# Other read orders behind four groups of head matmuls, and a later second use of x's first block

## The chip, the cores and the metric

The kernel runs on one core of one Trainium2 chip. The metric is the time of one execution in device microseconds (us); the time given for a kernel is the median of its runs. A profile is one execution, recorded by the hardware profiler; its span goes from the first to the last instruction.

## The reference

A trunk of one attention layer with a residual and two RMS norms, in float32, for x of 256 rows and 4096 columns, 32 heads of 128. (The second, convolutional layer of the file is not reached: DEPTH is 1.)

```python
h = x
xn = rms_norm(h, norm_attn)
q, k, v, g = split(xn @ w_in_attn, 4)          # 4096 x 16384
# per head, strictly causal, scale = 1/sqrt(128):
z = q @ k.T * scale
log_fail = where(causal, log_sigmoid(-z), 0)
suffix = reverse_cumsum(log_fail) - log_fail
a = where(causal, exp(log_sigmoid(z) + suffix), 0)
o = a @ v
h = h + (o * silu(g)) @ w_out_attn              # 4096 x 4096
out = rms_norm(h, final_norm)
```

## The kernel before, in words

The two large products are cut into units. The 16 units of the first (u = 0 to 15) each hold 256 columns of q, k, v and gate, so two heads; the units behind them hold the columns of the output product. A unit goes through 16 steps of 256 rows of the weights. In a step a scheme of Strassen's kind, with seven block products in place of eight in some steps, is applied; unit 0 and the first output unit use plain blocks (eight). Each block product is three matmuls of 512 columns in a rounded float32 (`mm3`): the operands are split into a high and a low part, and high x high, high x low and low x high are added up in one PSUM bank. The weights' parts are made per step, the high by a cast on ScalarE (`wh`), the low by a subtraction on VectorE (`wl`, line of `piece`). The parts of x (`forms`, `sh` and `sl`) are made once in unit 0 for that unit's plain blocks (`blocks_of`) and extended there by sums of blocks for the mixed units (`sums_of`).

`mm3` takes for each of the three matmuls a letter. The letter says in which order the 512 columns of the moving operand are read and those of the bank written: "e" reads runs of eight columns, 32 columns apart, in four passes; "c" reads runs of four, 16 apart, in four passes; three letters are a word, the word of one product. All orders give the same sum for each column. Which word a product gets is decided in `product`: the first products behind a group of other matmuls take the words of a list, one after the other; apart from that the first product of a step takes "ecc", and every other "eee".

The groups of other matmuls are those of the heads. A head has four: turn (transposes of q and k), scores, scan (the running sums) and values, two heads to a unit, in the order turn, scores, scan, values of head 0, then of head 1. They are put between the products of the next unit as soon as their inputs are there. In the middle of the run the products that follow them up to the next group are 3 (turn 0), 9 (scores 0), 9 (scan 0), 4 (values 0), 4 (turn 1), 8 (scores 1), 8 (scan 1) and 72 (values 1).

The order of instructions on each engine is written out when the kernel is built, by a planner (`Plan`) that simulates the engines: work asks for an engine with a cost and a key (its due time), the engine takes the waiting work with the lowest key when it is free, and what it takes is emitted in that order. So the order within an engine is fixed and a late instruction holds up those behind it. All instructions therefore show one line in the profile, L135; they are told apart by the names of their tiles. `yield nc.until(name)` lets a piece of planned work sleep until another has told that name: it changes the order, and adds no semaphore by itself.

For x's first block (i = 0) `blocks_of` makes the high and low forms in two cuts, since the first products wait for them. Then it scales the block by the gain (2 ScalarE instructions of 256 columns), subtracts its halves (256 columns on VectorE) and splits the differences into two parts (`differences`, `both_parts`), for use from unit 1 on; with that the block's buffer ("one") is given back, and the load of block 4 can take it. The name ("low", 2, 0) is told when the low of part 2, the first part of step 1 of unit 0, is planned to be done.

Of the kernel before, what the change touches and what calls it, by code (L numbers as in the profile page):

```python
# [19 lines left out]
P = 128  # L20
# [7 lines left out]
NB = D // CW  # L28
# [6 lines left out]
RUNS = {"e": (4, 8), "c": (4, 4), "g": (2, 8)}  # L35
BEHIND_OTHERS = ("ccc", "ecc", "eee", "eee", "eee", "eee", "ecc")
IN_STEP = ("ecc", "ecc")
BEHIND = {}
WARM, WARM_SHORT, IDLE = 10, 5, 640


# [70 lines left out]
def tensor_ns(n):  # L112
    return 0.4167 * n + 8.5 if n > 128 else 109.0
# [138 lines left out]
def kernel(  # L252
# [10 lines left out]
    nc = Plan(tc)  # L263
# [14 lines left out]
    def minus(out_, full, part):  # L278
        nc.vector.tensor_tensor(out=out_, in0=full, in1=part.bitcast(F32), op=ALU.subtract)
# [49 lines left out]
    def soon(c=4.0):  # L329
        return nc.here + 1e3 * c  # L330
# [13 lines left out]
    FULL_P, FULL_S = (P,) * 2, (W,) * 2  # L344

    since_others, words = 0, BEHIND_OTHERS

    def ten(emit, *n, what):
        def others():
            nonlocal since_others, words  # L350
            first_ = BEHIND.get(what, ())
            since_others, words = 0, first_ + BEHIND_OTHERS[len(first_) :]
            emit()

        return nc.work("tensor", 40 + sum(tensor_ns(m) for m in n), others, nc.here - 1e4, wait=400)
# [209 lines left out]
    def blocks_of(i):  # L565

        key = place_of[0, i]
        tag = ("one", "two", "s", "s")[i % 4]
        yield nc.take(tag)
        pool, inside, bufs = (wp, "s", SINGLES) if tag == "s" else (ap, tag, 1)  # L570
        y = pool.tile([P, KT, S], F32, tag=inside, name=f"xs{i}", bufs=bufs)
        y4 = y.rearrange("p k (a b) -> p (k a) b", a=NT)
        h, l = new_forms(i, "s")
        gain = lambda c: gcol[:, i * KT + c : i * KT + c + 1]
        if i:
            yield moved(
                "sync", lambda: nc.sync.dma_start(y, xT[i]), [KT * S], key - 1, hold=True, wait=1300 * i - 600 if i < 4 else 0
            )

            def scaled():  # L580
                for c in range(KT):
                    nc.scalar.activation(y[:, c, :], y[:, c, :], AF.Copy, scale=gain(c))
                nc.scalar.copy(h[:, 0:4, :], y4)

            yield act(scaled, (S, S, 2 * S), key - 2e3)
            yield dve(lambda: minus(l[:, 0:4, :], y4, h[:, 0:4, :]), 2 * S, key)
        else:
            yield moved("scalar", lambda: nc.scalar.dma_start(gcol, gain_in), [KC], key - 1)
            yield moved("scalar", lambda: nc.scalar.dma_start(y, xT[i]), [KT * S], key - 1, hold=True)
            for c in range(KT):  # L590
                hc, lc = (t[:, 2 * c : 2 * c + 2, :].rearrange("p a b -> p (a b)") for t in (h, l))

                yield dve(
                    lambda: nc.vector.tensor_scalar(out=hc, in0=y[:, c, :], scalar1=gain(c), scalar2=None, op0=ALU.mult),
                    S, key - 1,
                )
                nc.tell(("sh", c))
                yield nc.until(("low", 0, c))
                yield dve(
                    lambda: nc.vector.scalar_tensor_tensor(  # L600
                        out=lc, in0=y[:, c, :], scalar=gain(c), in1=hc.bitcast(F32), op0=ALU.mult, op1=ALU.subtract
                    ),
                    S, key - 1,
                )
        nc.tell(("form", "s", i))
        later = place_at(0, i + BLOCKS_LATER)
        if not i:

            def scaled():
                for c in range(KT):  # L610
                    nc.scalar.activation(y[:, c, :], y[:, c, :], AF.Copy, scale=gain(c))

            yield act(scaled, (S, S), later)
        yield from sums_of(i, y4, "n", later)
        nc.give(tag)
# [214 lines left out]
    BW = 3 * P  # L830
    not_before = off.broadcast_to([P, 2, P])

    def head(u, i):
        act_ = lambda *w: act(*w, soon(4.0 if u else HEADS_FIRST))
        yield nc.take("att", "gh", sooner=True)
        tr = att.tile([P, 2, S], F32, tag="att", name=f"tr{u}_{i}")

        def turn():
            for k in range(2):
                for t in range(NT):  # L840
                    c = k * CW + i * P
                    nc.tensor.transpose(tr[:, k, t * P : (t + 1) * P], st["qk", u][:, t, c : c + P], ident)

        yield ten(turn, P, P, P, P, what=("turn", i))
        if i == HG - 1:
            nc.give("one")
        qk = wp.tile([P, 2, S], F32, tag="gh", name=f"qkT{u}_{i}", bufs=ROWS)
        yield act_(lambda: nc.scalar.copy(qk, tr), 2 * S)
        nc.give("att")
        yield nc.take("att", sooner=True)  # L850
        bank = att.tile([P, W], F32, tag="att", name=f"z{u}_{i}")
        z, gT = bank[:, 0:BW], bank[:, BW:W]

        def turned(to, t):
            nc.tensor.transpose(to, st["gv", u][:, t, i * P : (i + 1) * P], ident)

        def scores():
            kw = dict(stop=False, skip_group_check=True)
            nc.tensor.matmul(z[:, 0:P], qk[:, 1, P:S], qk[:, 0, P:S], start=True, **kw)
            nc.tensor.matmul(z[:, P:BW], qk[:, 1, 0:P], qk[:, 0, :], start=False, **kw)  # L860
            diagonal = z[:, 0 : 2 * P].rearrange("p (a b) -> p a b", a=2)
            nc.tensor.matmul(diagonal, ident_b, not_before, start=False, **kw)

        yield ten(scores, *FULL_P, *FULL_S, 2 * P, what=("scores", i))
        nc.give("gh")
        yield nc.take("gh", sooner=True)

        f = wp.tile([P, BW], F32, tag="gh", name=f"f{u}_{i}", bufs=ROWS)

        def soft():  # L870
            nc.scalar.activation(f, z, AF.Softplus, scale=scale)
            nc.scalar.activation(f, f, AF.Copy, scale=1.0 / scale)

        yield act_(soft, (BW + TABLE, BW))
        yield nc.take("gh", "gh", sooner=True)
        fh, fl = (wp.tile([P, BW], F32R, tag="gh", name=f"f{k}{u}_{i}", bufs=ROWS) for k in "hl")
        yield act_(lambda: nc.scalar.copy(fh, f), BW)
        yield dve(lambda: minus(fl, f, fh), BW)
        nc.give("gh")

        if i == 0:
            yield nc.until(("gate", u))

        def scan():
            kw = dict(start=False, skip_group_check=True)
            nc.tensor.matmul(z, neg_tri, fh, stop=False, **kw)
            nc.tensor.matmul(z, neg_tri, fl, stop=False, **kw)
            nc.tensor.matmul(z[:, 2 * P : BW], neg_one, fh[:, 0:P], stop=False, **kw)
            nc.tensor.matmul(z[:, 2 * P : BW], neg_one, fl[:, 0:P], stop=True, **kw)
            turned(gT, 0)  # L890

        yield ten(scan, BW, BW, P, P, P, what=("scan", i))
        nc.give("gh", "gh")
        gated = st["gv", u][:, :, i * P : (i + 1) * P]
        yield nc.take("gh", sooner=True)
        a = wp.tile([P, BW], F32, tag="gh", name=f"a{u}_{i}", bufs=ROWS)


        def weights_of():
            nc.scalar.activation(a, z, AF.Relu, scale=-scale)  # L900
            nc.scalar.activation(a, a, AF.Exp, scale=-1.0)

        yield act_(weights_of, (BW, BW + TABLE))
        yield act_(lambda: nc.scalar.copy(gated[:, 0, :], gT), P)
        nc.give("att")
        yield nc.take("att", sooner=True)
        bank2 = att.tile([P, BW], F32, tag="att", name=f"o{u}_{i}")
        o, gT2 = bank2[:, 0:S], bank2[:, S:BW]
        v = lambda t: st["gv", u][:, t, CW + i * P : CW + (i + 1) * P]

        def out_of_head():
            kw = dict(skip_group_check=True)
            nc.tensor.matmul(o, v(0), a[:, P:BW], start=True, stop=False, **kw)
            nc.tensor.matmul(o[:, P:S], v(1), a[:, 0:P], start=False, stop=True, **kw)
            turned(gT2, 1)

        yield ten(out_of_head, *FULL_P, *FULL_S, P, what=("values", i))
        nc.give("gh")
        yield act_(lambda: nc.scalar.copy(gated[:, 1, :], gT2), P)
        o2 = o.rearrange("p (t b) -> p t b", t=NT)  # L920
        yield dve(lambda: nc.vector.tensor_tensor(out=gated, in0=o2, in1=gated, op=ALU.mult), S)
        nc.give("att")
# [444 lines left out]
```

## Time and profile before

| what | value |
|---|---|
| median of 3 runs | 1682.7 us (1682.67 to 1683.74) |
| the profiled execution's own time | 1683.75 us |
| its span | 1681.7 us |
| TensorE (PE) busy | 1666.9 us, 99% |
| VectorE (DVE) busy | 1611.1 us, 96% |
| ScalarE (ACT) busy | 1265.1 us, 75% |
| mean DMA rate | 249 GB/s |
| mean granted TensorE clock | 0.997 |

Matmuls are pipelined: the time from one's start to the next's is shorter than the duration of one in its row, so the pace is read from the starts. Rows name the tiles: `acc` are the products, `tr`, `z` and `o` the heads' matmuls, `xs` x's blocks, `sh` and `sl` their forms, `raw`, `wh` and `wl` the weights and their parts. A bracket behind a row says how long the engine stood idle before it and what released it. The letters of the words are not in the rows; they follow from the code.

### The profile page before, as it was taken

To read this page: it belongs to the slowest core of one execution; us is meant where nothing else is said; L and a number is where in the kernel's file an instruction comes from. 1 tells how busy PE (TensorE), PEld (TensorE's weight loads), DVE (VectorE), ACT (ScalarE), POOL (GpSimd) and SP (SyncE) were. 2 spreads that over 40 slices of the span, in tenths; PEclk is the share of its full clock that TensorE was granted. 3 is DMA by queue.
4 is the path that set the end of the run, shared out by engine and by line. 5 is a ranking of instruction groups with operands and counts; after the bars stand their busy time and mean duration, and the time that the engine had idled before them with its cause. 6 is when DMAs were issued, how large, how long until landed. Compare 5 with 4: busy or idle time off the path is not lost.

```text
span 1681.7 us, 25051 instructions
## 1 busy us (share of the span) xinstructions
PE 1666.9 (99%) x7736; PEld 1410.1 (84%) x7736; DVE 1611.1 (96%) x1851; ACT 1265.1 (75%) x1665; POOL 366.0 (22%) x448
## 2 busy tenths in 40 slices
PE   9999999999999999999999999999999999999997
PEld 7888888888888888888888888888888888888885
DVE  9899999999999999999999999999999978999997
ACT  8896868686868696968686868686878766665664
POOL 0022222222222222222222221222222112212110
PEclk9999999999999999999999999999999999999998
DMA  9978898989897989797989897979898978888895
GB/s 340 350 187 255 228 253 226 263 221 261 225 265 212 271 209 279 199 282 200 278 204 279 216 265 214 260 225 255 229 249 233 290 252 251 268 251 269 254 313 189
DMA packets 254325, 419.31 MB, mean 249 GB/s; under 512 B 28912, under 2 KB 77296, under 8 KB 254192
## 3 DMA queue, kind: packets, MB, share of 16 engines
q1 hardware_dynamic: 195696, 356.34, 63.8%
q0 software_dynamic: 58208, 61.11, 21.8%
q8 instruction: 60, 0.98, 0.3%
q14 instruction: 73, 0.60, 0.1%
q10 hardware_dynamic: 288, 0.28, 0.1%
HBM read 408.17 MB, written 9.44 MB: 248 GB/s over the span
## 4 chain that ended last, share of the span: by engine, by line
PE 98%; DVE 1%; DMA 0%; ACT 0%; issue 0%; SPq 0%; DVEq 0%; ACTq 0%
PE acc L135 93%; PE z L135 3%; PE o L135 1%; PE tr L135 1%; DMA raw<-in_w_in_dram 0%; DVE wl L135 0%; DVE h L135 0%; ACT xs L135 0%; DVE xs L135 0%; SPq L135 0%; ACT sq L135 0%; ACT wh L135 0%; DVE wh L135 0%; DVE scalars L135 0%; ACT scalars L135 0%
## 5 line engine op out<-in xcount | busy, mean ns | idle before, releaser
L135 ACT CAST wh<-raw 128x1024 fp32r<-128x1024 f32 (+1 forms) x1019 | 935.8, 965 | 315.4 <-PE acc L135 131.3
L135 DVE TENSOR_TENSOR wl<-raw,wh 128x1024 fp32r<-128x1024 f32 (+1 forms) x830 | 991.6, 1221 | 35.5 <-PE acc L135 12.7
L135 PE MATMUL acc<-wh,sh 128*128 128x512 f32 x2048 | 767.1, 388 | 0.0
L135 PE MATMUL acc<-wh,sl 128*128 128x512 f32 x1883 | 721.7, 383 | 0.0
L135 PE MATMUL acc<-wl,sh 128*128 128x512 f32 x1718 | 655.1, 381 | 1.1 <-DVE wl L135 1.1
L135 POOL DMA_DIRECT2D raw<-in_w_in_dram x330 | 284.0, 942 | 1000.9 <-DMA raw<-in_w_in_dram 333.0
L135 PEld LDWEIGHTS acc<-wh,sh 128*128 128x128 f32 x2048 | 384.7, 188 | 67.9 <-ACT sh L135 0.5
L135 PEld LDWEIGHTS acc<-wh,sl 128*128 128x128 f32 x1883 | 353.1, 188 | 64.4 <-DVE sl L135 0.4
L135 PEld LDWEIGHTS acc<-wl,sh 128*128 128x128 f32 x1718 | 322.5, 188 | 57.8 <-DVE wl L135 1.9
L135 DVE TENSOR_TENSOR raw<-raw 128x512 f32<-128x512 f32 x378 | 361.0, 955 | 4.3 <-DMA raw<-in_w_in_dram 1.2
L135 PE MATMUL acc<-wh,oh 128*128 128x512 f32 x512 | 193.0, 384 | 0.2
L135 PE MATMUL acc<-wh,ol 128*128 128x512 f32 x488 | 186.9, 383 | 0.0
L135 PE MATMUL acc<-wl,oh 128*128 128x512 f32 x464 | 177.2, 382 | 0.0
L135 DVE TENSOR_TENSOR wh<-raw,wh 128x512 fp32r<-128x512 f32 x189 | 130.0, 688 | 1.7 <-ACT wh L135 1.7
L135 PEld LDWEIGHTS acc<-wh,oh 128*128 128x128 f32 x512 | 96.0, 187 | 18.7 <-DVE h L135 0.9
L135 PEld LDWEIGHTS acc<-wh,ol 128*128 128x128 f32 x488 | 91.5, 187 | 16.4
L135 ACT ACT_TABLE_LOAD x81 | 103.9, 1283 | 1.4
L135 PEld LDWEIGHTS acc<-wl,oh 128*128 128x128 f32 x464 | 87.0, 187 | 16.3 <-DVE wl L135 0.7
L135 POOL DMA_DIRECT2D raw<-in_w_out_dram x48 | 41.7, 967 | 172.8 <-DVE wl L135 49.6
L135 POOL DMA_DIRECT2D p<-spill x28 | 17.7, 654 | 88.0 <-DVE ol L135 50.7
L135 DVE SCALAR_TENSOR_TENSOR gv_sb<-acc,scalars,gv_sb 128x512 f32<-128x512 f32 x45 | 33.8, 750 | 0.0
L135 ACT CAST oh<-p 128x512 fp32r<-128x512 f32 (+3 forms) x47 | 21.3, 470 | 14.8 <-DVE p L135 12.7
(89 smaller groups left out, 713.4 us busy)
## 6 DMA issues: line engine op xcount, KB each, us to landing
raw<-in_w_in_dram SPq DMA_DIRECT2D x1024, 256.0 KB, 4.4
raw<-in_w_out_dram SPq DMA_DIRECT2D x256, 256.0 KB, 4.8
raw<-in_w_in_dram POOLq DMA_DIRECT2D x330, 128.0 KB, 5.0
p<-spill POOLq DMA_DIRECT2D x28, 256.0 KB, 4.3
raw<-in_w_out_dram POOLq DMA_DIRECT2D x48, 128.0 KB, 5.8
xr<-in_x_dram SPq DMA_DIRECT2D x16, 256.0 KB, 5.3
spill<-gv_sb POOLq DMA_DIRECT2D x32, 128.0 KB, 4.5
xres<-in_x_dram SPq DMA_DIRECT2D x16, 256.0 KB, 5.9
```

The costliest lines, as they stand in the source:

```text
L135: return self.tc.keep_in_program_order(getattr(self.engine, name)(*args, **kw))
```

## The change

Behind four of the eight groups of a unit (scores 0, scan 0, values 0 and turn 1), the list of words is replaced for the heads of units 1 to 14; units 0 and 15 and the other four groups keep the old list. To tell the units apart, the name that `ten` gets has u in front. Second, the scaling of x's first block and what follows from it there sleep until ("low", 2, 0) is told.

| group | words before | words after |
|---|---|---|
| scores 0 | ccc ecc eee eee eee eee ecc | cec eee eee eee eee eee ecc |
| scan 0 | ccc ecc eee eee eee eee ecc | ccc eee eee eee eee eee ecc |
| values 0 | ccc ecc eee eee eee eee ecc | eee eee ecc eee eee eee ecc |
| turn 1 | ccc ecc eee eee eee eee ecc | eee ecc eee eee eee eee ecc |

```diff
-BEHIND = {}
+BEHIND = {
+    ("scores", 0): ("cec", "eee", "eee", "eee", "eee", "eee", "ecc"),
+    ("scan", 0): ("ccc", "eee", "eee", "eee", "eee", "eee", "ecc"),
+    ("values", 0): ("eee", "eee", "ecc", "eee", "eee", "eee", "ecc"),
+    ("turn", 1): ("eee", "ecc", "eee", "eee", "eee", "eee", "ecc"),
+}
...
     def ten(emit, *n, what):
         def others():
             nonlocal since_others, words
-            first_ = BEHIND.get(what, ())
-            since_others, words = 0, first_ + BEHIND_OTHERS[len(first_) :]
+            u, *group = what
+            words = BEHIND.get(tuple(group), BEHIND_OTHERS) if 0 < u < NB - 1 else BEHIND_OTHERS
+            since_others = 0
             emit()
...
         if not i:
+            yield nc.until(("low", 2, 0))
 
             def scaled():
...
-        yield ten(turn, P, P, P, P, what=("turn", i))
+        yield ten(turn, P, P, P, P, what=(u, "turn", i))
```

(`scores`, `scan` and `values` get u in the same way.)

More of the change, by code (lines that the diff above doesn't have):

```diff
@@ L862, in scores @@
             nc.tensor.matmul(diagonal, ident_b, not_before, start=False, **kw)
-        yield ten(scores, *FULL_P, *FULL_S, 2 * P, what=("scores", i))
+        yield ten(scores, *FULL_P, *FULL_S, 2 * P, what=(u, "scores", i))
         nc.give("gh")
@@ L890, in scan @@
             turned(gT, 0)
-        yield ten(scan, BW, BW, P, P, P, what=("scan", i))
+        yield ten(scan, BW, BW, P, P, P, what=(u, "scan", i))
         nc.give("gh", "gh")
@@ L915, in out_of_head @@
             turned(gT2, 1)
-        yield ten(out_of_head, *FULL_P, *FULL_S, P, what=("values", i))
+        yield ten(out_of_head, *FULL_P, *FULL_S, P, what=(u, "values", i))
         nc.give("gh")
```

## The prediction

> **What bounds the kernel now.** I read the page's busy times and its chain of waits first, to see which engine sets the end.
>
> ```profile
> PE 1666.9 (99%) x7736; PEld 1410.1 (84%) x7736; DVE 1611.1 (96%) x1851; ACT 1265.1 (75%) x1665; POOL 366.0 (22%) x448
> ...
> PE 98%; DVE 1%; DMA 0%; ACT 0%; issue 0%; SPq 0%; DVEq 0%; ACTq 0%
> ```
>
> TensorE is the chain for 98% of the span of 1681.7 us. What can move the time is therefore the spacing of its matmuls, and the few places where it stands still. The second view is the chain in order of time, around one unit in the middle of the run. Columns: start us, us, what, number of instructions.
>
> ```profile
> 841.12 2.01 PE acc L135 x9
> ...
> 843.90 6.01 PE acc L135 x27
> ...
> 850.58 5.98 PE acc L135 x27
> ...
> 857.32 2.68 PE acc L135 x12
> ...
> 860.44 2.69 PE acc L135 x12
> ...
> 863.89 5.36 PE acc L135 x24
> ...
> 869.91 5.33 PE acc L135 x24
> ...
> 876.00 47.67 PE acc L135 x216
> ```
>
> Each row is the run of products behind one small group of a head's matmuls: head 0's turn, scores, scan and values, then head 1's. The change touches the second to the fifth row (scores 0, scan 0, values 0, turn 1). The same eight rows come in every unit, about 83 us apart.
>
> Now the pace inside a run. These are the first and the last of 14 product matmuls in an undisturbed stretch, in the timeline of TensorE (start us, us, instruction):
>
> ```profile
> 168.65 0.38 PE L135 MATMUL acc<-wh,sh 128*128 128x512 f32 x1
> ...
> 171.51 0.38 PE L135 MATMUL acc<-wl,sh 128*128 128x512 f32 x1
> ```
>
> 13 intervals in 2.86 us are 0.220 us each. There is a slower pace too. Here are the first and the last of 11 matmuls, all read eight wide ("e"), that follow a standstill of TensorE:
>
> ```profile
> 35.55 0.39 PE L135 MATMUL acc<-wh,sl 128*128 128x512 f32 x1
> ...
> 37.86 0.39 PE L135 MATMUL acc<-wh,sh 128*128 128x512 f32 x1
> ```
>
> 10 intervals in 2.31 us are 0.231 us each: the same instruction, the same operands' kinds, 0.011 us more, and it goes on for as long as only "e" is read. So after a disturbance the stream can settle at 0.220 or at 0.231 us, and the words decide which. That is what the change plays with.
>
> What the words cost now, in the run behind scores 0, read "ccc", "ecc", "eee", "eee" and on:
>
> ```profile
> 843.97 0.39 PE L135 MATMUL acc<-wl,sh 128*128 128x512 f32 x1
> 844.20 0.38 PE L135 MATMUL acc<-wh,sl 128*128 128x512 f32 x1
> 844.42 0.39 PE L135 MATMUL acc<-wh,sh 128*128 128x512 f32 x1
> 844.64 0.38 PE L135 MATMUL acc<-wl,sh 128*128 128x512 f32 x1
> ...
> 845.09 0.39 PE L135 MATMUL acc<-wh,sh 128*128 128x512 f32 x1
> 845.33 0.39 PE L135 MATMUL acc<-wl,sh 128*128 128x512 f32 x1
> 845.56 0.39 PE L135 MATMUL acc<-wh,sl 128*128 128x512 f32 x1
> 845.79 0.38 PE L135 MATMUL acc<-wh,sh 128*128 128x512 f32 x1
> ```
>
> From 843.97 to 845.79 there are 8 intervals, 1.82 us against 1.76 at 0.220. The three from 845.09 on are slow, then the pace is right.
>
> **The change, part by part.** The *words*. Nothing is added or removed: the number of matmuls, their operands and their columns stay, only the order in which 512 columns are read and written. What can be won per unit is what the four rows of the chain hold above 0.220 us per matmul: scores 0 6.01 - 27 x 0.220 = 0.07, scan 0 5.98 - 5.94 = 0.04, values 0 2.68 - 2.64 = 0.04, turn 1 2.69 - 2.64 = 0.05 us. About 0.05 of the sum of 0.20 stays whatever is read (the step's own "ecc" inside the long rows, and the first matmul's remainder), so the lower bound is -0.15 us a unit. The filter takes units 1 to 14, so 14 times: -2.1 us.
>
> *Scan 0* ("ccc", then "eee" instead of "ecc") has the best evidence:
>
> ```profile
> 850.64 0.38 PE L135 MATMUL acc<-wl,sh 128*128 128x512 f32 x1
> ...
> 851.31 0.38 PE L135 MATMUL acc<-wl,sh 128*128 128x512 f32 x1
> ...
> 851.99 0.38 PE L135 MATMUL acc<-wl,sh 128*128 128x512 f32 x1
> ```
>
> The three steps from 850.64 take 0.67 us, those from 851.31, the second pair of "c", 0.68. The second pair repeats the first, so the stream has its pace after the first, and leaving it out saves 0.68 - 0.66 = 0.02. I take -0.02. Upper bound: the first pair doesn't suffice and 15 matmuls up to the next "ecc" run at 0.231, 15 x 0.011 = +0.16.
>
> *Scores 0* ("cec", then "eee") has two "c" with an "e" between them where there were five. No row shows a lone "e" between two "c". Lower bound -0.05, upper bound again 15 x 0.011 = +0.16. The nearest row is the present one, where the three slow matmuls at 845.09 come behind the second pair, which goes; I take -0.04.
>
> *Values 0* ("eee", "eee", "ecc") and *turn 1* ("eee", "ecc") begin with "e". Behind a group no row shows that; behind a standstill the rows from 35.55 show 0.231. Upper bounds: values 0 has 6 slow intervals, 6 x 0.011 = 0.066, then a pair of "c" that brings the pace back at up to scores 0's 0.07, less the 0.04 paid now: +0.10. Turn 1 has 3 slow intervals, +0.03, and its pair in place of the present ones. Lower bounds -0.03 and -0.04. For turn 1 the present words show what the pair costs:
>
> ```profile
> 860.95 0.38 PE L135 MATMUL acc<-wh,sh 128*128 128x512 f32 x1
> 861.17 0.39 PE L135 MATMUL acc<-wl,sh 128*128 128x512 f32 x1
> 861.40 0.40 PE L135 MATMUL acc<-wh,sl 128*128 128x512 f32 x1
> 861.64 0.39 PE L135 MATMUL acc<-wh,sh 128*128 128x512 f32 x1
> ```
>
> The pair from 861.17 takes 0.23 and 0.24, and the same pair stays in the new words. A group is not a standstill: TensorE works through it and its weight loads run ahead, so I don't take the upper ends. Between the ends I take +0.01 for values 0 and -0.01 for turn 1.
>
> Sum: -0.02 - 0.04 + 0.01 - 0.01 = -0.06 us a unit, times 14 = **-0.8 us**. The upper ends of all four are +0.45 a unit, +6.3 us.
>
> The Trainium skill ("TensorE: Matmul & The Clock Gate", the step-by-step part on LDWEIGHTS and the section "Back-to-back issue gap") says that the weight load and the moving operand have read ports of their own and gives N / 2.4 + 2.5, which is 216 ns for 512 columns whatever the order. By that the words would be worth nothing and the sum would be 0; the trace's 0.220 and 0.231 for one instruction disagree with it.
>
> *x's first block.* Its scaling (2 on ScalarE) and the subtraction and two castings behind it move behind the second step's first low.
>
> ```profile
> 9.07 0.90 ACT L135 ACTIVATE xs<-xs,gcol 128x256 f32<-128x256 f32 x2
> ...
> 10.00 1.61 DVE L135 TENSOR_TENSOR xs<-xs 128x256 f32<-128x256 f32 x5
> 11.53 1.22 DVE L135 TENSOR_TENSOR wl<-raw,wh 128x1024 fp32r<-128x1024 f32 x1
> ...
> 11.75 0.39 PE L135 MATMUL acc<-wh,sh 128*128 128x512 f32 x1
> 12.80 0.50 PE L135 MATMUL acc<-wl,sh 128*128 128x512 f32 x1 [0.67 <-DVE wl L135]
> ```
>
> TensorE stands still from 11.97 to 12.80, 0.83 us, for the low at 11.53. Without the 0.90 us of scaling ahead of it the high is cast up to 0.8 us earlier; without the first of the five subtractions (256 of their 768 columns, so 0.4 to 0.5 of the 1.61 us) the low comes 0.4 us earlier, since the other four (block 1's) stay ahead of it. So 0.4 us of the stall goes, 0.83 at most. But it is not kept. The next standstill, and VectorE up to it:
>
> ```profile
> 33.62 0.40 PE L135 MATMUL acc<-wh,sl 128*128 128x512 f32 x1
> 34.04 0.50 PE L135 MATMUL acc<-wh,sh 128*128 128x512 f32 x1
> ...
> 35.10 0.38 PE L135 MATMUL acc<-wh,sh 128*128 128x512 f32 x1
> ```
>
> ```profile
> 14.00:34.00 20.00, 20.00 (x91) 16.67 (x89) 19.67 (x36) 17.22 (x31) 0.00 (x0) 1.00 1.02 358
> ```
>
> In the last row the third pair is VectorE: 19.67 of 20.00 us. It does the same work before 34 us in either order, so the form for which TensorE waits at 34.04 comes when it came, and a TensorE that is 0.4 us early waits 0.4 us longer. I take 0 for this edit. Upper bound: behind the new wait are one scaling, one subtraction, a cast, a low and the release of the block's buffer, for which this load waits:
>
> ```profile
> 16.42 0.33 SPq L135 DMA_DIRECT2D xs<-in_xT_dram  x1
> ```
>
> It is block 4's, wanted at about 28.6 us (12.80 + 3 x 24 x 0.220). If it slips behind the next raw loads it still lands in time. A slip that puts block 0's 0.8 us of VectorE work ahead of the form at 34 costs up to +0.8. Lower bound -0.83.
>
> **The rivals.** *R1, the slow pace holds* (slower): "e" behind a group settles at 0.231. Place: the matmuls behind scores 0, values 0, turn 1. For it: the rows from 35.55. Against it: behind scan 0 and turn 1 an "e" within four matmuls runs at 0.220 (860.95 to 861.17). Price (0.16 + 0.10 + 0.03 - 0.02) x 14 = +3.8, 1686.5 us; it decides once scores 0 runs slow to the next step. *R2, all of it settles at once, and what follows too* (faster): -0.15 for the four, and scores 1, scan 1 and values 1, which stand 0.08, 0.05 and 0.15 above 0.220, begin in a better phase and give back 0.12 more: -0.27 x 14 = -3.8, 1678.9. For it: the rows behind scan 0 and scan 1 differ with the same words, so what came before matters. Against: their words are not changed. *R3, the start decides*: the 0.83 us stay won, 1681.1 with the words, or the form at 34 comes 0.8 late, 1682.7. *R4, the words are worth nothing*, the skill's rule as a mechanism: 1682.7, against which both paces speak.
>
> **How the numbers follow.** The profiled execution took 1683.75 us with a span of 1681.7, the runs 1682.67 to 1683.74, median 1682.7; it is the upper edge of them, and I put the difference of -0.8 to the median: **1681.9 us**. Within 0.2% (3.4 us, about what a measurement of this kernel can tell from no change) are all cases but the far ones. Chances: the forecast 0.62, R1 0.13, R2 0.10, R3 0.10, R4 0.05. R1 lies a little beyond 0.2%, so 0.08 of it count as slower and 0.05 as same; of R2 0.08 count as faster. The rest is the same: 0.84. Range: -2.1 for the four words' lower bound up to part of R1, +3.3: 1679.6 to 1685.2.
>
> **What would show it.** In the chain's rows of the changed kernel, 6.01 behind scores 0 becomes about 5.97, 5.98 about 5.96, 2.68 and 2.69 stay within 0.02. At 6.15 or more R1 is right. Rows 5.36, 5.33 and 47.67 that fall by over 0.03 speak for R2. The idle of 0.67 for the low at 12.80 shrinks to some 0.3 and the standstill near 34 grows by as much; if it doesn't grow, R3. I'm wrong above all if a run behind a changed group is longer than now.

## The result and the profile after

The changed kernel takes 1686.57 us (median of 13 runs, 1685.19 to 1687.91) against 1682.7 us before (median of 13 too, 1680.82 to 1684.09): ratio 1.0023, 95% interval 1.0014 to 1.0031. It is slower, by 3.9 us. The forecast was 1681.9, the range ended at 1685.2, and the rival R1 had priced its loss at +3.8 us with a chance of 0.13.

The page of the changed kernel, busy times and chain, shows the same bound (its lines carry L140 where those of before carry L135):

```profile
PE 1669.8 (99%) x7736; PEld 1409.4 (84%) x7736; DVE 1611.6 (96%) x1851; ACT 1265.2 (75%) x1665; POOL 366.1 (22%) x448
...
PE 97%; DMA 1%; DVE 1%; issue 0%; ACT 0%; SPq 0%; DVEq 0%; ACTq 0%
```

TensorE has 2.9 us more busy time with the same 7736 matmuls; the span is 1684.7 against 1681.7 us. Where these lie is seen in the chain of waits in order of time, for the same unit as in the prediction (start us, us, what, count):

```profile
842.74 2.04 PE acc L140 x9
...
845.54 6.22 PE acc L140 x27
...
852.42 6.03 PE acc L140 x27
...
859.21 2.66 PE acc L140 x12
...
862.30 2.70 PE acc L140 x12
...
865.77 5.36 PE acc L140 x24
...
871.79 5.33 PE acc L140 x24
...
877.88 47.66 PE acc L140 x216
```

Behind scores 0 stands 6.22 where 6.01 stood: +0.21 us. Turn 0, whose words are not changed, has 2.04 for 2.01; scan 0 6.03 for 5.98; values 0 2.66 for 2.68; turn 1 2.70 for 2.69. These rounded rows add up to +0.28 us. From one unit's turn 0 to the next one's it is 83.24 us for 82.99, +0.25 us, and from turn 0 of unit 1 to turn 0 of unit 15, 14 units on, 3.5 us more (1167.35 for 1163.81). All else is small.

The timeline of TensorE inside the run behind scores 0, now read "cec", "eee", "eee" and on; the first and the last of the 21 matmuls that follow the first two words:

```profile
846.75 0.39 PE L140 MATMUL acc<-wh,sh 128*128 128x512 f32 x1
...
851.37 0.40 PE L140 MATMUL acc<-wh,sl 128*128 128x512 f32 x1
```

20 intervals in 4.62 us are 0.231 us: the slow pace of the prediction, and it is kept to the end of the run, through the list's "ecc" (the three matmuls from 849.52 on). The clock is not the cause: the granted clock is 1.00 in this stretch and 1.00 from 880 to 920 us, where the pace is 0.220.

At the start the standstill for the second step's first low has shrunk, and a new one stands at the fifth step:

```profile
12.21 0.39 PE L140 MATMUL acc<-wh,sh 128*128 128x512 f32 x1
12.60 0.49 PE L140 MATMUL acc<-wl,sh 128*128 128x512 f32 x1
```

```profile
28.72 0.38 PE L140 MATMUL acc<-wl,sh 128*128 128x512 f32 x1
29.40 0.49 PE L140 MATMUL acc<-wh,sl 128*128 128x512 f32 x1 [0.30 <-DVE sl L140]
```

0.39 us from one start to the next where it was 1.05, and 0.68 where an undisturbed interval is 0.22. The standstills near 34 us, which cost 0.6 us before (from 33.62 to 35.10 in place of 4 x 0.22), are gone. In this profile head 0's turn of unit 0 begins at 91.85 us for 92.19.

### The profile page after: what moved, and what is told of

Same layout as the page of the kernel before. It is cut to its first block, busy times and chain, and to the rows that moved or that the text cites. A ratio compares the mean times of both kernels' runs of the same rounds, so it can differ in the third digit from the quotient of the medians.

```text
span 1684.7 us, 25052 instructions
## 1 busy us (share of the span) xinstructions
PE 1669.8 (99%) x7736; PEld 1409.4 (84%) x7736; DVE 1611.6 (96%) x1851; ACT 1265.2 (75%) x1665; POOL 366.1 (22%) x448
## 4 chain that ended last, share of the span: by engine, by line
PE 97%; DMA 1%; DVE 1%; issue 0%; ACT 0%; SPq 0%; DVEq 0%; ACTq 0%
PE acc L140 92%; PE z L140 3%; DMA raw<-in_w_in_dram 1%; PE o L140 1%; PE tr L140 1%; DVE wl L140 0%; DVE h L140 0%; ACT sq L140 0%; SPq L140 0%; DVE sl L140 0%; DVE wh L140 0%; DVE scalars L140 0%; ACT scalars L140 0%; DVE h_back L140 0%; DVE raw L140 0%
## 5 line engine op out<-in xcount | busy, mean ns | idle before, releaser
L140 ACT CAST wh<-raw 128x1024 fp32r<-128x1024 f32 (+1 forms) x1019 | 935.9, 965 | 315.3 <-PE acc L140 134.1
L140 DVE TENSOR_TENSOR wl<-raw,wh 128x1024 fp32r<-128x1024 f32 (+1 forms) x830 | 990.0, 1218 | 40.6 <-ACT wh L140 15.1
L140 PE MATMUL acc<-wh,sh 128*128 128x512 f32 x2048 | 768.1, 388 | 0.5 <-DVE sh L140 0.5
L140 PE MATMUL acc<-wh,sl 128*128 128x512 f32 x1883 | 723.1, 384 | 0.3 <-DVE sl L140 0.3
L140 PE MATMUL acc<-wl,sh 128*128 128x512 f32 x1718 | 656.6, 382 | 0.6 <-DVE wl L140 0.4
L140 POOL DMA_DIRECT2D raw<-in_w_in_dram x330 | 284.3, 948 | 1004.1 <-DMA raw<-in_w_in_dram 360.7
L140 PEld LDWEIGHTS acc<-wh,sh 128*128 128x128 f32 x2048 | 384.6, 188 | 69.4 <-ACT wh L140 0.6
L140 PEld LDWEIGHTS acc<-wh,sl 128*128 128x128 f32 x1883 | 353.0, 187 | 66.0 <-DVE sl L140 1.1
L140 PEld LDWEIGHTS acc<-wl,sh 128*128 128x128 f32 x1718 | 322.6, 188 | 58.4 <-DVE wl L140 2.0
L140 DVE TENSOR_TENSOR raw<-raw 128x512 f32<-128x512 f32 x378 | 359.4, 951 | 2.7 <-DMA raw<-in_w_out_dram 0.6
L140 PE MATMUL acc<-wh,oh 128*128 128x512 f32 x512 | 192.8, 384 | 0.2
L140 PE MATMUL acc<-wh,ol 128*128 128x512 f32 x488 | 186.7, 383 | 0.0
L140 PE MATMUL acc<-wl,oh 128*128 128x512 f32 x464 | 177.3, 382 | 0.0
L140 DVE TENSOR_TENSOR wh<-raw,wh 128x512 fp32r<-128x512 f32 x189 | 129.1, 683 | 1.4 <-ACT wh L140 1.4
L140 PEld LDWEIGHTS acc<-wh,oh 128*128 128x128 f32 x512 | 96.0, 187 | 18.5 <-DVE h L140 0.9
L140 PEld LDWEIGHTS acc<-wh,ol 128*128 128x128 f32 x488 | 91.5, 187 | 16.3
L140 PEld LDWEIGHTS acc<-wl,oh 128*128 128x128 f32 x464 | 87.0, 187 | 16.9 <-DVE wl L140 1.5
L140 POOL DMA_DIRECT2D raw<-in_w_out_dram x48 | 41.6, 954 | 172.0 <-DVE wl L140 51.2
L140 POOL DMA_DIRECT2D p<-spill x28 | 17.6, 650 | 88.9 <-DVE ol L140 50.9
L140 ACT CAST oh<-p 128x512 fp32r<-128x512 f32 (+3 forms) x47 | 21.3, 469 | 17.1 <-DVE p L140 12.7
L140 DVE SCALAR_TENSOR_TENSOR gv_sb<-acc,scalars,gv_sb 128x512 f32<-128x512 f32 x45 | 33.4, 743 | 0.0
```

Source lines behind the costliest of these rows:

```text
L140: return self.tc.keep_in_program_order(getattr(self.engine, name)(*args, **kw))
```

## The experiments

Theory A after the result: the new words behind scores 0 leave the stream at the slow pace. Rivals: B, the new order at the start costs it; C, the lists that begin with "e" (values 0, turn 1) cost it.

**The words without the wait.**

```diff
-            yield nc.until(("low", 2, 0))
```

> The four new lists of words, without the wait at the start. Theory A (the words behind scores 0 leave the stream at the slow pace): as slow as the whole change, 0.2 to 0.25% over the kernel before (+3.4 to +4.2 us), the chain's row behind scores 0 at 6.2 us against 6.01. Rival B (the new order at the start, with standstills of TensorE at 6.7 and 28.7 us, costs the time): no difference from the kernel before, within 0.05%.

Measured: 1686.85 us, ratio 1.0020 (1.0011 to 1.0029). (A ratio here compares all executions of a kernel with those of the kernel before in the same session, whose medians were 1682.7 to 1683.1 us; it isn't the quotient of two of the medians given.)

**The wait without the words.**

```diff
-    ("scores", 0): ("cec", "eee", "eee", "eee", "eee", "eee", "ecc"),
-    ("scan", 0): ("ccc", "eee", "eee", "eee", "eee", "eee", "ecc"),
-    ("values", 0): ("eee", "eee", "ecc", "eee", "eee", "eee", "ecc"),
-    ("turn", 1): ("eee", "ecc", "eee", "eee", "eee", "eee", "ecc"),
```

> The wait at the start alone, all words as before. Theory A: within 0.05% of the kernel before; the first head group begins 0.3 us earlier (91.9 us against 92.2), as in the changed kernel. Rival B: 0.2% slower.

Measured: 1683.06 us, ratio 0.9995 (0.9985 to 1.0004). B falls: the words carry the loss. The first head group began at 92.2 us in this profile, as in that of the kernel before, so the 0.3 us seen in the changed kernel doesn't come back in each. All profiles of this document together lean to a small gain: the group begins at 91.9 to 92.3 us in the seven with the wait and at 92.2 to 93.0 in the nine without, 0.6 us earlier on the mean, of which 0.3 us stand already at the first product, ahead of the edit. In the times, which differ by several us from one execution to the next, the start is worth nothing that these runs can tell.

**Without the list behind scores 0, and that list alone.**

```diff
-    ("scores", 0): ("cec", "eee", "eee", "eee", "eee", "eee", "ecc"),
```

> The change with the old words behind scores 0, so three of the four lists and the wait. Theory A: the loss is gone, -0.5 to +0.5 us against the kernel before, rows behind scores 0 near 6.01, values 0 near 2.66, turn 1 near 2.70. Rival C (the lists that begin with e, behind values 0 and turn 1, cost it): +1.5 us or more stays.

> The kernel before with the new list behind scores 0 alone. Theory A: 14 x 0.21 = +2.9 us behind scores 0 and up to 14 x 0.05 = +0.7 behind scan 0, which then begins at the slow pace: +2.9 to +3.6 us, ratio 1.0017 to 1.0021; row behind scores 0 at 6.2. Rival C: under +1 us.

Without it: 1682.68 us, ratio 0.9996 (0.9987 to 1.0004); C falls with that. (In its rows turn 0 is at 2.04, scores 0 at 5.99, scan 0 at 6.03.) Alone, in the kernel before and without the wait, as all kernels with single lists below: 1683.35 us, ratio 0.9997 (0.9989 to 1.0006). Theory A, as it was put, falls too: taking the list out removes the loss, but adding it alone makes none. The chain's rows of the kernel with this list alone, behind turn 0 and scores 0, first in unit 1, then in unit 7:

```profile
177.77 2.03 PE acc L137 x9
180.57 6.22 PE acc L137 x27
...
675.77 2.01 PE acc L137 x9
678.54 5.98 PE acc L137 x27
```

The same words give 6.22 us in one unit and 5.98, 0.03 better than before, in another. The row of turn 0 ahead of it differs as well, 2.03 and 2.01. So it matters how the stream arrives at scores 0. I call that the phase of arrival; its mark in the chain is turn 0's row, 2.01 us before the change and 2.04 in the changed kernel. (It is a mark, no measure: 2.03 and 2.06 occur too, mostly in unit 1.) Something in the change moves it a unit ahead. Theory D: the words behind turn 1 do. Rival E: those behind scan 0 or values 0.

**Without turn 1's list; turn 1's list alone; scores 0 and turn 1 together.**

```diff
-    ("turn", 1): ("eee", "ecc", "eee", "eee", "eee", "eee", "ecc"),
```

> The change without the new words behind turn 1 (scores 0, scan 0, values 0 and the wait stay). Theory D (the words behind turn 1 shift the phase in which the next unit's turn 0 and scores 0 begin, and in that phase cec does not bring the pace back): scores 0's row stays near 5.97 us, as with scores 0's words alone, turn 0 as before, values 0 gains 0.02; in all -0.05 us a unit or more, some -0.7 to -1 us (ratio 0.9993 to 0.9997). Rival E (the words behind scan 0 or values 0 shift it): scores 0's row at 6.2 us and +3 us or more (ratio 1.0018).

> The kernel before with the new words behind turn 1 alone. Theory D: the run behind turn 0 in the units from 2 on is 0.03 us longer than before (0.03 x 13 = 0.4 us), as in the changed kernel, while scores 0 with its old words is not slow (at most 6.01). Rival E: turn 0's run as before.

> The kernel before with the new words behind scores 0 and turn 1, and nothing else. Theory D: scores 0's row at 6.2 us in every unit, +0.2 x 14 = +2.9 to +3.7 us. Rival E: 5.97 us from unit 2 on, and no loss.

Without turn 1's list the loss stays: 1685.9 us, ratio 1.0016 (1.0007 to 1.0025). The rows behind turn 0 and scores 0, unit 7:

```profile
676.48 2.04 PE acc L139 x9
679.29 6.22 PE acc L139 x27
```

Theory D falls and E stands. Scores 0 and turn 1 together (one execution, 1681.21 us) gain behind scores 0, turn 1 and scores 1, and no row of the middle units is longer; turn 0, scores 0, scan 0, values 0, turn 1 and scores 1 in unit 7:

```profile
675.28 2.01 PE acc L138 x9
...
678.05 5.98 PE acc L138 x27
...
684.70 5.98 PE acc L138 x27
...
691.44 2.68 PE acc L138 x12
...
694.56 2.66 PE acc L138 x12
...
697.98 5.34 PE acc L138 x24
```

Turn 1 alone has the same mark, 2.01 behind turn 0, with 2.65 behind turn 1 for 2.69 and 5.34 behind scores 1 for 5.36. Its one time was 1686.3 us all the same; in its trace TensorE loses 0.3 us around turn 0 in units 1 and 2 and 0.9 us in unit 14, where the chain leaves TensorE for ScalarE's copy of the turned heads (`qkT`) before the scores. Such delays came at single places of other runs too, the part from turn 0 of unit 15 to the end took 338.1 to 343.5 us in the profiles of this document (341.8 here), and executions of the kernel before reached 1686.4 us in the same session. So one time is no verdict, and the rows, which repeat to 0.01 us, carry the argument.

One of these delays is a test by itself. In unit 13 of the changed kernel without the wait TensorE stood still at turn 0 and again ahead of the scores. The same words in the same kernel, 6.22 us behind scores 0 in units 1 to 12 and 14, are there at

```profile
1180.45 5.98 PE acc L140 x27
```

**Values 0's list alone, scan 0's alone, and the change without values 0's.** Theory F: values 0's words move the phase of arrival. Rival G: scan 0's do.

```diff
-    ("values", 0): ("eee", "eee", "ecc", "eee", "eee", "eee", "ecc"),
```

> The kernel before with the new words behind values 0 alone. Theory F (these words move the phase in which all later groups arrive): values 0 gains 0.02 us, but scan 1, values 1 and the next unit's turn 0 change without new words of their own: turn 0's run 0.03 us longer, scores 0 with its old words no longer at 6.01 but 0.025 less, as in the kernel without scores 0's list. Rival G (scan 0's words do it): turn 0's run as before.

> The kernel before with the new words behind scan 0 alone. Theory F: the run behind scan 0 is 0.01 to 0.02 us shorter, all other rows as before. Rival G: turn 0's run 0.03 us longer and values 0 and turn 1 changed too.

> The change without the new words behind values 0 (scores 0, scan 0, turn 1 and the wait stay). Theory F: scores 0 gains 0.03 from unit 2 on, turn 1 0.035, scores 1 0.025 and scan 0 some 0.01 us: about 0.1 us a unit, 0.2 us lost in unit 1, so -1.0 to -1.4 us against the kernel before (ratio 0.9992 to 0.9994), and 5 us less than the change. Rival G: scores 0's row at 6.2 us, +2.5 to +3 us.

The rows behind turn 0, scores 0, scan 0 and values 0 in unit 7, first with values 0's list alone:

```profile
675.33 2.04 PE acc L137 x9
...
678.14 5.99 PE acc L137 x27
...
684.79 6.01 PE acc L137 x27
...
691.55 2.66 PE acc L137 x12
```

and with scan 0's alone:

```profile
675.83 2.01 PE acc L137 x9
...
678.61 6.01 PE acc L137 x27
...
685.28 5.96 PE acc L137 x27
```

Values 0's words (one execution, 1682.29 us) take 0.02 us off their own run and bring 2.04 behind the next unit's turn 0; scores 0 with its old words goes from 6.01 to 5.99, and scan 0 with its old words from 5.98 to 6.01. Scan 0's (one execution, 1682.54 us) leave 2.01 and gain 0.02. The change without values 0's list takes 1681.45 us, ratio 0.9995 (0.9987 to 1.0004), 5 us less than the change. F holds, though scan 1 and values 1, which it expected to change too, differ by 0.01 us at most. The rows behind turn 0, scores 0, scan 0, values 0 and turn 1 in unit 7:

```profile
674.63 2.01 PE acc L139 x9
...
677.40 5.98 PE acc L139 x27
...
684.05 5.96 PE acc L139 x27
...
690.76 2.68 PE acc L139 x12
...
693.88 2.65 PE acc L139 x12
```

So each of the four lists alone shortens the run behind it in the middle of the kernel (scores 0 by 0.03, scan 0 by 0.02, values 0 by 0.02, turn 1 by 0.03 to 0.04 and scores 1 behind it by 0.02 us); with values 0's among them scores 0's costs 0.21, scan 0's 0.05, and turn 1's gain is gone. The whole of a unit shows it best, from one turn 0 to the next (median over units 2 to 12):

| new lists | unit, us | against before |
|---|---|---|
| none (before) | 82.99 | |
| scores 0 alone | 82.95 | -0.03 |
| scan 0 alone | 82.96 | -0.03 |
| values 0 alone | 82.98 | -0.01 |
| turn 1 alone | 82.93 | -0.06 |
| scores 0 and turn 1 | 82.89 | -0.09 |
| all four (the change) | 83.24 | +0.25 |
| all but scores 0 | 83.01 | +0.03 |
| all but turn 1 | 83.23 | +0.24 |
| all but values 0 | 82.87 | -0.12 |

The single lists add up to -0.13 us, and without values 0's to -0.12, which is what those three together give; the four together give +0.25. Taking out either scores 0's or values 0's list removes all or nearly all of the loss, so it belongs to the two together. (No kernel had these two and no others in every unit.)

**The same fourteen lists behind scores 0 in both phases.** One list in each of units 1 to 14, once with all other words old, once with the new words behind values 0 in every unit (one execution each, 1684.33 and 1685.28 us).

```diff
+                words = TRIED[u] if tuple(group) == ("scores", 0) else BEHIND.get(tuple(group), BEHIND_OTHERS)
```

> The kernel before, with another list behind scores 0 in each of units 1 to 14, otherwise old words: (first two products, then eee unless said) 1 ccc eee, 2 cec eee, 3 ecc eee, 4 cce eee, 5 eec eee, 6 eee eee, 7 cec ecc, 8 cce ecc, 9 eee ecc, 10 ecc ecc, 11 ccc cce, 12 eee eee ecc, 13 cec cec, 14 ccc eee ecc. If what counts is whether a pair of c stands side by side, units 3, 4, 9 and 12 keep the pace (row up to 6.05 us) and units 5 and 6 are slow (6.15 us or more). If it is the phase of arrival alone, whole lists with a pair of c are slow too, and some without one are not.

> The fourteen lists of the other survey behind scores 0, one a unit, now with the new words behind values 0 in all units, so that scores 0 is reached in the other phase. If the phase of arrival decides, the same lists give other lengths: cec eee slow (6.2 us, it was 5.97 in the first phase), and others of those that were slow in the first phase (ccc eee, ecc eee, eee eee) change by 0.05 us or more. If the list decides, every unit from 3 on gives the length of the first survey within 0.02 us.

The row behind scores 0 in units 3, 5, 6, 9 and 12 ("ecc eee", "eec eee", "eee eee", "eee ecc", "eee eee ecc"), old words elsewhere:

```profile
347.00 6.16 PE acc L151 x27
...
513.28 5.96 PE acc L151 x27
...
596.21 6.16 PE acc L151 x27
...
845.30 6.16 PE acc L151 x27
...
1094.52 6.04 PE acc L151 x27
```

and with the new words behind values 0:

```profile
346.99 5.99 PE acc L151 x27
...
513.17 6.14 PE acc L151 x27
...
596.28 5.94 PE acc L151 x27
...
845.60 5.97 PE acc L151 x27
...
1094.86 5.94 PE acc L151 x27
```

The list that was best in the one phase ("eec eee", 5.96) is slow in the other (6.14), and three that were slow (6.16) are now at 5.94 to 5.99. That a pair of "c" must stand side by side is refuted by both: "eee eee" keeps the pace in the second phase without any "c", "ecc eee" loses it in the first with one. So neither the list nor the phase decides alone: which lists keep the pace depends on the phase. The expectation's "cec eee" (unit 2) is slow in the second survey, 6.22 with 2.04 behind turn 0; its 5.97 belongs to the kernel with scores 0's list alone, since unit 2 of the first survey arrives with 2.06 and is at 6.22 as well. (In unit 6 of the second survey turn 0's row was 2.03, not 2.04; the others named had 2.04, and 2.01 in the first survey.)

**Two versions from the rows.**

```diff
-    ("scores", 0): ("cec", "eee", "eee", "eee", "eee", "eee", "ecc"),
-    ("values", 0): ("eee", "eee", "ecc", "eee", "eee", "eee", "ecc"),
+    ("scores", 0): ("eec", "eee", "eee", "eee", "eee", "eee", "ecc"),
...
-            words = BEHIND.get(tuple(group), BEHIND_OTHERS) if 0 < u < NB - 1 else BEHIND_OTHERS
+            first_u = 1 if group[0] == "turn" else 2
+            words = BEHIND.get(tuple(group), BEHIND_OTHERS) if first_u <= u < NB - 1 else BEHIND_OTHERS
```

That is the second; the first has no list behind scan 0 either. Unit 1 is left out since it arrives in another phase.

> A version put together from the rows: turn 1's new words in units 1 to 14, eec eee behind scores 0 in units 2 to 14, old words behind scan 0 and values 0, and the wait. By the rows of single lists: turn 1 0.035, scores 1 0.025, scores 0 0.053 us a unit less, 14 x 0.06 + 13 x 0.053 = -1.5 us (ratio 0.9991). If the gains depend on each other more than these rows show, less or a loss.

> A version from the rows of the single lists: turn 1's new words in units 1 to 14, scan 0's new words and eec eee behind scores 0 in units 2 to 14, old words behind values 0, and the wait. Sum by rows: turn 1 and scores 1 0.060, scores 0 0.053, scan 0 0.027 us a unit: 14 x 0.060 + 13 x 0.080 = -1.9 us (ratio 0.9989), all rows as in the single ones. If the arrivals shift again, scores 0's row goes to 6.1 us or more.

The first takes 1680.94 us, ratio 0.9992 (0.9983 to 1.0001); the second 1680.93 us, ratio 0.9988 (0.9979 to 0.9998), which beats the kernel before by 0.12% (0.02 to 0.21%), and the changed one by 5.6 us. (Its profiled execution took 1684.47 us all the same, the longest of the eleven: a unit is 82.85 us in it, but the part from unit 15 on took 343.5 us.) Its rows in unit 7 behind turn 0, scores 0, scan 0, values 0, turn 1 and scores 1:

```profile
674.31 2.01 PE acc L139 x9
...
677.08 5.96 PE acc L139 x27
...
683.71 5.96 PE acc L139 x27
...
690.42 2.68 PE acc L139 x12
...
693.54 2.65 PE acc L139 x12
...
696.96 5.34 PE acc L139 x24
```

The single gains add up: 5.96, 5.96, 2.65 and 5.34 are those of the runs with one list. How much hangs on the arrival shows in unit 13 of the first version, where TensorE stood still ahead of the scores; the row behind scores 0 that follows, with the same "eec", is

```profile
1175.14 6.14 PE acc L138 x27
```

and 5.96 in units 2 to 12. (Unit 10 is among these, with 2.06 behind turn 0.)

## Why the prediction was wrong

**What bounds it: right.** TensorE's spacing was the time, there are two paces, 0.220 and 0.231 us, and the words, together with the arrival, decide between them. The price of one slow interval, 0.011 us, was right. The upper bound of +0.16 for scores 0 was not: it counted 15 matmuls up to the next "ecc", and in the change the slow pace goes through that "ecc" to the end of the run, so +0.21 against the old row was measured.

**The step that failed** is "scores 0, I take -0.04", and behind it the assumption that the four lists can be priced one by one, each from the row of its own group, and added. Alone the list does give -0.03 from unit 2 on. In the change it gives +0.21, since values 0's list, one unit ahead, changes the phase in which turn 0 and scores 0 are reached. Turn 0, which the sum left out because its words stay, adds +0.03. R2 carried the clue ("the rows behind scan 0 and scan 1 differ with the same words, so what came before matters"), and it was used only for a gain. (The two rows named are a thin example: above 0.220 us per matmul they stand 0.04 and 0.05. Scores 0's 0.07 against scan 0's 0.04, with the same words, shows it better.) The same clue allows a loss in each of the four rows, and the upper ends that the prediction had worked out (+6.3 us in all) belonged in the range. The range doesn't follow from its own terms either: -2.1 and R1's +3.8, counted from 1682.7, give 1680.6 and 1686.5, not 1679.6 and 1685.2.

**R1: near in its price by luck, right in one of its three places, wrong in its cause.** It gave 1686.5 us, +0.27 us a unit, with scores 0, values 0 and turn 1 slow because an "e" behind a group settles at 0.231. The rows measured come to +0.28 from other parts: scores 0 +0.21 where R1 had +0.16, scan 0 +0.05 for -0.02, turn 0 +0.03 for nothing, values 0 -0.02 for +0.10, turn 1 +0.01 for +0.03. Scores 0 is slow to the end of its run, but its list begins with "c"; values 0, which begins with two words of "e", holds 0.220 us and gains 0.02; turn 1 has 2.70 for 2.69. The rows behind a standstill, from which an "e" behind a group was feared to be slow, don't carry over: behind scores 0 "eee eee" is at 6.16 in one phase and at 5.94 in the other.

**Values 0 +0.01 and turn 1 -0.01:** measured -0.02 and +0.01 in the change. **Scan 0 -0.02:** -0.02 alone, +0.05 in the change.

**The start, 0: not refuted in the time, wrong in its steps.** The wait alone is at 0.9995 (0.9985 to 1.0004). The standstill near 34 was to grow by what the first one lost; it vanished, which by the prediction's own sign speaks for R3, a gain that stays. Of the 1.3 us that the two standstills give in this profile, 0.6 go at another place, the fifth step's form at 28.72 us, 0.3 at 6 to 7 us, ahead of the edit, and 0.1 at 18 us; 0.3 are left at the first head group. So the zero is in part luck. The slip of block 4's load that the prediction named as the way to a loss fits that place: in the changed kernel the load is issued at 18.93 us for 16.42, and VectorE makes two of the weights' lows ahead of the form's last low parts, which begin at 28.66 us, where one low stood ahead of those at 27.36. No run here takes the two apart.

**R4, that the words are worth nothing,** is refuted by the rows of the survey: 5.96 against 6.16 us for 27 matmuls that differ in their words alone, both with 2.01 behind turn 0. The Trainium skill ("TensorE: Matmul & The Clock Gate", the step-by-step part on LDWEIGHTS) has the weight load and the moving operand on read ports of their own, so that a load takes no read bandwidth from the running matmul. It says nothing there of an order of reading; that the words are then worth nothing was the prediction's reading, and the rows disagree with it. A word sets the order of reading the moving operand and of writing the bank together, so no run tells which of the two matters.

What stays open is what the phase is in the chip, and by what way through the groups between them values 0's words reach the next unit's turn 0: the rows behind scan 1 and values 1 differ by no more than 0.01 us.

## What to carry to other kernels

Where a stream of matmuls can settle at more than one pace, edits that only shift its rhythm are not priced one by one: each sets how the next place is reached, so test a list in the company it will have, and look for a mark of the arrival (here 2.01 or 2.04 us behind an unchanged group) ahead of the row itself. When several small edits together lose while none loses alone, take them out one at a time from the whole as well as adding them one at a time to the old kernel: where taking out either of two removes the loss, it belongs to the pair. A spot that repeats in every unit can be surveyed with another variant in each repetition of one run, as long as the arrival stays the same from one to the next.

## What the runs showed of the hardware

A stream of these matmuls of 128x512 runs at 0.220 or 0.231 us from start to start with the same kinds of operands and the same order of reading and writing, at a granted clock of 1.00 in both. The slow pace lasted 20 intervals to the end of a run in the changed kernel, through an "ecc"; in unit 6 of the first survey ("eee eee", 6.16 us) the last five intervals, behind the "ecc", are at 0.22 again. Which pace follows a group depends on the words and on how the stream arrives, and a difference of 0.03 us in an unchanged row ahead goes with it. Fourteen lists gave lengths of 5.96 to 6.20 us for 27 matmuls in the first survey, units 3 to 14, and 5.94 to 6.22 in the second.
